# A two-layer attention and retention trunk on one core: gate chunk ahead of the attention, decay tiles two steps sooner, one up chunk in halves, and low weight parts from ScalarE and an accumulating DMA

## The chip, the core and the metric

The kernel runs on one core of a Trainium2 chip. The metric is the device time of the whole program in microseconds (us), as the median of several runs. Engines are named as in the profile: PE is TensorE (PEld is its weight load, which overlaps the matmuls), DVE is VectorE, ACT is ScalarE, POOL is GpSimd, and SP is SyncE, which here only issues DMAs.

## What is computed

Two layers work on a residual stream `h` of 512 tokens by 1024 features, all in float32. Cut to what matters, with the parts that the change touches in full width:

```python
u = rms_norm(h, norm_mix_pre[i])
qa, ka, va, qr, kr, vr, gr, gate_a, gate_b = split(u @ w_in[i])
att = dilated_attention_mixer(qa, ka, va)          # 8 heads of 64, softmax over banded keys
ret = retention_mixer(qr, kr, vr, gr, decay[i])    # 8 heads, decay matrix, group norm, silu(gr) gate
merged = sigmoid(gate_a) * (att @ w_att_out[i]) + sigmoid(gate_b) * (ret @ w_ret_out[i])
h = h + rms_norm(merged @ w_out[i], norm_mix_post[i])
u = rms_norm(h, norm_mlp_pre[i])
h = h + rms_norm(square(relu(u @ w_mlp_up[i])) @ w_mlp_down[i], norm_mlp_post[i])
gate = sigmoid(rms_norm(h) @ w_ple_gate[i])
h = h + gate * rms_norm(p[i] @ w_ple_proj[i], norm_ple[i])
```

## The kernel before

**Products in three terms.** Every float32 operand of a large product is split into a high part (a cast to the matmul's 32-bit format) and a low part (the operand minus its high part), and each product is the sum of high by high, high by low and low by high (`HL`, L292). Weights come as chunks of 128 by 1024 elements (512 KB) in the order of `PLAN_LAYER` (L69). `prefetch` (L268) loads a chunk into a `raw` tile over SP, casts the high part on ACT (L275), and takes the low part as a subtraction on DVE, or on POOL for two of three chunks of the kinds in `POOL_LOW` (the attention's and retention's q and k, retention's v, the gates `g` and `ga`, and the attention's output weights `ao`), as two instructions of 512 columns (L278). By the program there are 59 such chunks. `chunk` (L286) asks for the item three places ahead, and there are five `wt` buffers, so a tile's split can begin when PE starts the job four places ahead of its own.

**PE's order is written by hand.** PE executes in the order of the code; on DVE, ACT and POOL a scheduler sets the order by its own estimates and the priorities in `soon` (L372), and each engine then works strictly in that order. In the first half of a layer the main stream is a list of jobs, most of them 24 matmuls of 512 columns (`t_job`, L304): `rope_group` for q and k, `g_job` for the retention's gate, `vr_job`, `a_job` (gate of the attention and its output product), `b_gate`. The attention's and the retention's heads are a generator (`sides`, L728) that is advanced by `tick` (L469) at a rate of 0.94 for each 6 matmuls of the main stream; each `yield` is thus about one gap of 6 foreign matmuls. A head of the attention is four score steps (L543 to L550: PE, DVE, ACT's exponential, DVE's scaling of `z`), then the product of the head before (`pv`), then four steps of transposes of `z` (L562). A head of the retention is four score steps (L608 to L614), `finish` of the head before, the next head's decay tile `T` (`decay`, L581: POOL, then DVE, then ACT's exponential at L586), the product L630, its copy `yt` by ACT (L633), the transposes of `yt` on PE (L638) and the group norm on DVE and POOL.

**Norms.** `pre_norm` (L390) squares a token block of 128 (t0 to t3) on ACT (L348), takes the root on POOL (L356, L358), scales it on DVE (L404 or L407), and queues its transposes for PE: `step` (L322) emits them when the entry is `age` steps of 6 matmuls old, or `settle` does so when a product needs that block. ACT then casts the transposed block into `uT` (L415) and DVE makes the low part (L416). `AGE_DN` is the age in the down product. `EARLY` (L51) is how many chunks of the up product run as two halves of 256 token columns (L888), so that blocks t0 and t1 can start before t2 and t3 are normed.

The lines that the change touches most:

```python
AGE_DN = 6
EARLY = 3
            for sl in HALVES if pool else (slice(0, D),):
                low(nc.gpsimd if pool else nc.vector, t[:, 1, sl], r[:, sl], t[:, 0, sl])
```

## Time and profile before

| | before |
|---|---|
| median of 3 runs | 1790.33 us (1790.21 to 1791.44) |
| the profiled execution, whole | 1789.19 us |
| its span, first to last instruction | 1787.3 us |
| PE busy | 1771.2 us (99%) |
| DVE, ACT, POOL busy | 1138.5, 810.8, 374.9 us |
| granted TensorE clock | 1.000 |

PE is busy in nearly the whole span, so the time can only fall by PE's gaps or by matmuls that PE need not do. "Busy" counts from the start of a matmul to its modelled end, and neighbours overlap: 12 matmuls of 512 columns start 0.227 us apart, although one lasts 0.389 us. A wait shows its full length only between starts.

### The profile page before, as it was taken

What the parts mean: (1) busy time and instruction counts of PE and PEld (TensorE: products, weight loads), DVE (VectorE), ACT (ScalarE), POOL (GpSimd) and SP (SyncE); (2) the same over time, 40 slices, a digit from 0 to 9 for tenths busy, and PEclk for the clock granted to TensorE, in tenths of its full rate; (3) what the DMA queues carried; (4) which work ended last, traced back from release to release, by engine and by line L of the source; (5) the groups of instructions that cost most, each with busy time, mean ns of one, the idle gap of its engine ahead of it and who ended that gap; (6) DMA issues with size and microseconds to landing.
All of it is one profiled execution on the core that took longest, in us unless ns stands there. A gap on an engine that the chain in (4) does not pass through costs nothing.

```text
span 1787.3 us, 22085 instructions
## 1 busy us (share of the span) xinstructions
PE 1771.2 (99%) x8209; PEld 1465.5 (82%) x8209; DVE 1138.5 (64%) x1760; ACT 810.8 (45%) x1280; POOL 374.9 (21%) x346
## 2 busy tenths in 40 slices
PE   9999999999999999999999999999999999999998
PEld 7878888888898888888887888888888888888887
DVE  6677768743565677674656766677444657667754
ACT  5355554422466454433443555444234664444342
POOL 3321244311141001002123212443011410000030
PEclk9999999999999999999999999999999999999999
DMA  6554564552347566551346456556332566664411
GB/s 249 182 163 157 176 206 150 164 169 95 107 142 200 153 165 162 160 184 60 129 143 216 133 164 192 181 165 191 123 106 95 165 173 156 171 173 130 165 62 69
DMA packets 87951, 274.58 MB, mean 154 GB/s; under 512 B 11937, under 2 KB 20513, under 8 KB 87842
## 3 DMA queue, kind: packets, MB, share of 16 engines
q1 hardware_dynamic: 80930, 247.99, 41.4%
q0 software_dynamic: 6912, 25.17, 8.3%
q8 instruction: 65, 1.06, 0.2%
q14 instruction: 44, 0.36, 0.1%
HBM read 239.55 MB, written 33.55 MB: 153 GB/s over the span
## 4 chain that ended last, share of the span: by engine, by line
PE 91%; DVE 3%; POOL 2%; ACT 2%; DMA 1%; issue 1%; SPq 0%; POOLq 0%; ACTq 0%
PE acc L309 29%; PE acc L319 19%; PE s L309 18%; PE acc L866 9%; PE tp L866 4%; PE tp L630 2%; PE tp L525 2%; PE tp L562 2%; PE acc L888 1%; PE tp L412 1%; PE s L543 1%; PE s L608 1%; PE s L544 1%; PE s L609 1%; PE s L888 1%
## 5 line engine op out<-in xcount | busy, mean ns | idle before, releaser
L309 PE MATMUL acc<-uT,wt 128*128 128x512 f32 x1920 | 473.5, 393 | 0.0
L309 PEld LDWEIGHTS acc<-uT,wt 128*128 128x128 f32 x1920 | 355.8, 188 | 71.4
L298 DVE TENSOR_TENSOR wt<-raw,wt 128x1024 fp32r<-128x1024 f32 (+1 forms) x222 | 285.7, 1292 | 187.3 <-ACT wt L275 186.5
L275 ACT ACTIVATE wt<-raw 128x1024 fp32r<-128x1024 f32 x279 | 293.0, 1055 | 214.3 <-PE acc L309 109.1
L309 PE MATMUL s<-uT,wt 128*128 128x512 f32 x1392 | 323.7, 389 | 0.0
L319 PE MATMUL acc<-wt,uT 128*128 128x512 f32 x1320 | 319.0, 394 | 1.3 <-DVE wt L298 0.9
L309 PEld LDWEIGHTS s<-uT,wt 128*128 128x128 f32 x1392 | 261.1, 188 | 54.1
L319 PEld LDWEIGHTS acc<-wt,uT 128*128 128x128 f32 x1320 | 245.1, 188 | 52.6 <-DVE wt L298 2.3
L298 POOL TENSOR_TENSOR wt<-raw,wt 128x512 fp32r<-128x512 f32 x118 | 160.7, 1383 | 366.3 <-ACT wt L275 316.4
L866 PE MATMUL acc<-wt,op 128*128 128x512 f32 x672 | 159.5, 389 | 0.0
L866 PEld LDWEIGHTS acc<-wt,op 128*128 128x128 f32 x672 | 126.1, 188 | 26.2
L265 POOL DMA_DIRECT2D wsum<-in_w_dram x48 | 42.5, 891 | 418.9 <-DVE wt L298 140.2
L909 ACT ACTIVATE relu<-s 128x512 f32<-128x512 f32 x60 | 35.7, 594 | 182.9 <-PE s L309 173.6
L877 DVE TENSOR_TENSOR sumP<-acc,sumP 128x512 f32<-128x512 f32 x92 | 61.7, 686 | 56.8 <-PE acc L866 56.5
L309 PE MATMUL acc<-retT,wt 128*128 128x512 f32 x384 | 89.3, 389 | 0.0
L319 PE MATMUL acc<-wt,ff 128*128 128x512 f32 x384 | 88.5, 390 | 0.0
L298 DVE TENSOR_TENSOR wt<-wsum,wt 128x1024 fp32r<-128x1024 f32 x48 | 60.5, 1261 | 40.6 <-ACT wt L275 40.6
L309 PEld LDWEIGHTS acc<-retT,wt 128*128 128x128 f32 x384 | 72.1, 188 | 15.0
L319 PEld LDWEIGHTS acc<-wt,ff 128*128 128x128 f32 x384 | 71.8, 188 | 14.8
L301 ACT ACTIVATE rt<-rz 128x512 fp32r<-128x512 f32 x64 | 40.3, 631 | 91.2 <-DVE rz L612 91.0
L866 PE MATMUL tp<-wt,op 128*128 128x512 f32 x336 | 80.7, 389 | 0.0
L866 PEld LDWEIGHTS tp<-wt,op 128*128 128x128 f32 x336 | 63.1, 188 | 13.1
(164 smaller groups left out, 2149.2 us busy)
## 6 DMA issues: line engine op xcount, KB each, us to landing
raw<-in_w_dram SPq DMA_DIRECT2D x279, 512.0 KB, 3.7
wsum<-in_w_dram POOLq DMA_DIRECT2D x48, 512.0 KB, 5.5
kk<-stk SPq DMA_DIRECT2D x128, 128.0 KB, 4.5
wsum<-in_w_dram SPq DMA_DIRECT2D x24, 512.0 KB, 3.5
stq<-rr SPq DMA_DIRECT2D x16, 512.0 KB, 4.1
qs<-stq SPq DMA_DIRECT2D x128, 64.0 KB, 2.7
stk<-rr SPq DMA_DIRECT2D x16, 512.0 KB, 3.4
stv<-vr SPq DMA_DIRECT2D x16, 512.0 KB, 3.6
```

Source lines behind the costliest of these rows:

```text
L265: nc.gpsimd.dma_start(r, rows(src[1]), accum_op=ALU.add)
L275: nc.scalar.activation(t[:, 0, :], r, AF.Copy)
L298: eng.tensor_tensor(dst, src, hi.bitcast(F32), op=ALU.subtract)
L301: nc.scalar.activation(dst[:, 0], src, AF.Copy, scale=scale)
L309: nc.tensor.matmul(ps, lhsT=t[:, a, (off + k) * P:(off + k + 1) * P], rhs=r, start=k == 0 and n == 0, stop=k == kts - 1 and n == 2)
L319: nc.tensor.matmul(ps, lhsT=lhs(a, k, t), rhs=ch[:, b, j * S:(j + 1) * S], start=first and n == 0, stop=last and n == 2)
L525: nc.tensor.matmul(o, lhsT=v, rhs=pt[k][:, hl, :], start=k == 0 and hl == 0, stop=k == 3 and hl == 1)
L562: nc.tensor.transpose(ps[:, t * P:(t + 1) * P], zs[t][:, k * P:(k + 1) * P], ident)
L630: nc.tensor.matmul(o, lhsT=v[:, k, a * P:(a + 1) * P], rhs=rt[k][:, b, :], start=n == 0, stop=n == 11)
L866: nc.tensor.matmul(ps, lhsT=op[:, a, k, j * P:(j + 1) * P], rhs=t[:, b, k * S:(k + 1) * S], start=k == 0 and n == 0, stop=k == 1 and n == 2)
L877: nc.vector.tensor_tensor(a, ps, a, op=ALU.add)
L888: nc.tensor.matmul(early[c][:, 256 * j:256 * j + 256], lhsT=t[:, a, k * P:(k + 1) * P], rhs=uT[:, b, k, 256 * j:256 * j + 256], start=k == ...
```

## The change

Six edits:

- The low part of the 59 POOL chunks: ACT writes the negated cast of the weights into the low half of the tile, and a DMA issued by POOL adds the weights from HBM onto it. POOL's subtractions go, the chunks of DVE keep theirs.
- `g_job(0)` is called ahead of the start of the attention's generator, so 24 matmuls stand between the last rope product and the first score.
- Where an attention head has no earlier head to finish (head 0), one more `yield` is made.
- In the retention, `decay(h + 1)` is called at the second score step (k = 1) and no longer behind `finish`.
- `EARLY` goes from 3 to 1: the second and third up chunk run whole.
- `AGE_DN` goes from 6 to 7.

```diff
-AGE_DN = 6
+AGE_DN = 7
...
-EARLY = 3
+EARLY = 1
...
-            for sl in HALVES if pool else (slice(0, D),):
-                low(nc.gpsimd if pool else nc.vector, t[:, 1, sl], r[:, sl], t[:, 0, sl])
+            if pool:
+                nc.scalar.activation(t[:, 1, :], r, AF.Copy, scale=-1.0)
+                nc.gpsimd.dma_start(t[:, 1, :], rows(n).bitcast(F32R), accum_op=ALU.add)
+            else:
+                low(nc.vector, t[:, 1, :], r, t[:, 0, :])
...
             if late:
                 pv(*late)
+            else:
+                yield 1
...
                     qk, vh = load_qk(i, 1, h + 1), load_v(i, h + 1)
+                if k == 1 and h < 7:
+                    Tn = decay(h + 1)
                 yield 1
             if late:
                 finish(*late)
             yield 1
-            if h < 7:
-                Tn = decay(h + 1)
...
         rope_group(i, 0, 1, ca, "k")
+        g_job(0)
         side["gen"], side["rate"], side["owed"] = sides(), RATE, 0.0
...
         cr = cs_tile(1)
-        g_job(0)
         g_job(1)
```

Lines of the changed kernel stand 3 to 5 further down: L309 becomes L312, L348 L351, L404 L407, L415 L418, L416 L419, L543 L546, L562 L567, L586 L591, L633 L638; the negated cast is its L279 and the accumulating DMA its L280.

PE at head 0 of the attention in the first layer, from the last two score steps (L543, L544) to the first transposes (L562), before:

```order
L543 MATMUL s_81<-kk,qs 128x512
L544 MATMUL s_81<-kk,qs 128x512
L309 MATMUL acc_80<-uT,wt 128x512 x6
L543 MATMUL s_82<-kk,qs 128x512
L544 MATMUL s_82<-kk,qs 128x512
L309 MATMUL acc_80<-uT,wt 128x512 x12
L562 MATMUL tp_83<-ident,z 128x128 x4
```

And the same place in the changed kernel:

```order
L546 MATMUL s_81<-kk,qs 128x512
L547 MATMUL s_81<-kk,qs 128x512
L312 MATMUL acc_77<-uT,wt 128x512 x6
L546 MATMUL s_82<-kk,qs 128x512
L547 MATMUL s_82<-kk,qs 128x512
L312 MATMUL acc_77<-uT,wt 128x512 x18
L567 MATMUL tp_83<-ident,z 128x128 x4
```

Between the last score and the first transposes stand 18 foreign matmuls in place of 12.

ACT in the retention, from the third score's cast of a head (`rt`) to the copy `yt` that PE's transposes read, second head of the first layer, before:

```order
L301 ACTIVATE rt_2390<-rz_2388 128x512
L301 ACTIVATE rt_2404<-rz_2402 128x512
L301 ACTIVATE retT_2419<-yz_2417 128x512
L586 ACTIVATE T_2435<-T_2435 128x896
L633 ACTIVATE yt_2453<-tp1_84 128x512
```

And in the changed kernel, with the two casts of a chunk (L275, L279) ahead:

```order
L275 ACTIVATE wt_2551<-raw_2378 128x1024
L279 ACTIVATE wt_2551<-raw_2378 128x1024
L591 ACTIVATE T_2418<-T_2418 128x896
L304 ACTIVATE rt_2446<-rz_2444 128x512
L717 ACTIVATE tha_2449<-acc2_79 128x512
L304 ACTIVATE retT_2468<-yz_2466 128x512
L638 ACTIVATE yt_2490<-tp1_84 128x512
```

The decay tile's exponential no longer stands right ahead of `yt`; it is four places earlier, and a second cast has come in.

ACT in the down product of the first layer, second half: `un_6829` is the norm of block t1, `un_6885` that of t2, `junk` the square sum of t2, L275 casts of weights for the next product, and the casts into `uT` are first those of t0, then those of t1. Before:

```order
L415 ACTIVATE uT_88<-tp0_83 128x4x128
L415 ACTIVATE uT_88<-tp1_84 128x4x128
L348 ACTIVATE un_6829,ss_6831<-hr_6591 128x512
L348 ACTIVATE un_6829,ss_6834<-hr_6591 128x512
L348 ACTIVATE junk_6878,ss_6879<-sumP5_4440 128x512
L275 ACTIVATE wt_6755<-raw_6736 128x1024
L415 ACTIVATE uT_88<-tp0_83 128x4x128
L415 ACTIVATE uT_88<-tp1_84 128x4x128
L348 ACTIVATE un_6885,ss_6887<-hr_6593 128x512
L348 ACTIVATE un_6885,ss_6890<-hr_6593 128x512
```

And in the changed kernel, where `un_6781` is t1 and `un_6837` is t2:

```order
L351 ACTIVATE un_6781,ss_6783<-hr_6543 128x512
L418 ACTIVATE uT_88<-tp0_83 128x4x128
L351 ACTIVATE un_6781,ss_6786<-hr_6543 128x512
L418 ACTIVATE uT_88<-tp1_84 128x4x128
L351 ACTIVATE junk_6830,ss_6831<-sumP5_4440 128x512
L275 ACTIVATE wt_6707<-raw_6688 128x1024
L275 ACTIVATE wt_6718<-raw_6699 128x1024
L351 ACTIVATE un_6837,ss_6839<-hr_6545 128x512
L351 ACTIVATE un_6837,ss_6842<-hr_6545 128x512
L418 ACTIVATE uT_88<-tp0_83 128x4x128
L418 ACTIVATE uT_88<-tp1_84 128x4x128
```

The casts of t0 have moved between the halves of t1's norm, and those of t1 behind a second weight cast and the whole norm of t2.

DVE follows suit: at the same place the scaling of t1 (`un_6829`), then the square sum's operand of t2 (L950), the update of `h` for t2 (L943) and the low parts of t1's `uT`, before:

```order
L416 TENSOR_TENSOR uT_88<-tp1_84,uT_88 128x4x128
L404 TENSOR_SCALAR un_6829<-hr_6591,rstd_6836 128x512 x2
L950 TENSOR_TENSOR sumP5_4440<-acc0_77,sumP5_4440 128x512
L952 TENSOR_TENSOR sumP5_4440<-sumP5_4440,gain_4433 128x512
L943 SCALAR_TENSOR_TENSOR hr_6593<-sumP4_4444,rstd_6882,hr_6593 128x512
L943 SCALAR_TENSOR_TENSOR hr_6593<-sumP5_4440,rstd_6882,hr_6593 128x512
L416 TENSOR_TENSOR uT_88<-tp0_83,uT_88 128x4x128
L416 TENSOR_TENSOR uT_88<-tp1_84,uT_88 128x4x128
```

And in the changed kernel:

```order
L407 TENSOR_SCALAR un_6781<-hr_6543,rstd_6788 128x512 x2
L419 TENSOR_TENSOR uT_88<-tp1_84,uT_88 128x4x128
L955 TENSOR_TENSOR sumP5_4440<-acc2_79,sumP5_4440 128x512
L957 TENSOR_TENSOR sumP5_4440<-sumP5_4440,gain_4433 128x512
L948 SCALAR_TENSOR_TENSOR hr_6545<-sumP4_4444,rstd_6834,hr_6545 128x512
L948 SCALAR_TENSOR_TENSOR hr_6545<-sumP5_4440,rstd_6834,hr_6545 128x512
L301 TENSOR_TENSOR wt_6707<-raw_6688,wt_6707 128x1024
L301 TENSOR_TENSOR wt_6718<-raw_6699,wt_6718 128x1024
L407 TENSOR_SCALAR un_6837<-hr_6545,rstd_6844 128x512 x2
L419 TENSOR_TENSOR uT_88<-tp0_83,uT_88 128x4x128
L419 TENSOR_TENSOR uT_88<-tp1_84,uT_88 128x4x128
```

The low parts of t1's `uT` now stand behind two low parts of weights and the scaling of t2. The second layer has the same rows in the same order.

## Rows read from the trace of the kernel before

**Rows 1.** Page, part 1: busy us (share of the span), x instructions.
```profile
PE 1771.2 (99%) x8209; PEld 1465.5 (82%) x8209; DVE 1138.5 (64%) x1760; ACT 810.8 (45%) x1280; POOL 374.9 (21%) x346
```

**Rows 2.** Waits of PE, whole span: total us, times, longest.
```profile
PE tp L562 <- DVE z L550: 3.2, 4, 0.9
PE tp L638 <- ACT yt L633: 2.0, 5, 0.6
PE tp L412 <- DVE uT L416: 1.7, 2, 0.9
PE tp L412 <- DVE un L404: 1.6, 4, 0.6
...
PE s L543 <- DVE nm L547: 0.9, 2, 0.5
```

**Rows 3.** Timeline of PE, head 0, first layer: start, us, what, [idle before].
```profile
91.87 0.38 PE L562 MATMUL tp<-ident,z 128*128 128x128 f32 x2
...
94.42 1.64 PE L309 MATMUL acc<-uT,wt 128*128 128x512 f32 x6
95.89 0.60 PE L562 MATMUL tp<-ident,z 128*128 128x128 f32 x4
96.24 1.63 PE L309 MATMUL acc<-uT,wt 128*128 128x512 f32 x6
```

**Rows 4.** Timelines of DVE, then of POOL, there, and of DVE near 160.
```profile
89.93 0.48 DVE L550 TENSOR_SCALAR z<-z,rd 128x512 f32<-128x512 f32 x1
...
91.58 1.51 DVE L550 TENSOR_SCALAR z<-z,rd 128x512 f32<-128x512 f32 x1
...
90.19 2.61 POOL L298 TENSOR_TENSOR wt<-raw,wt 128x512 fp32r<-128x512 f32 x2 [4.74 <-ACT wt L275]
...
160.50 1.03 DVE L550 TENSOR_SCALAR z<-z,rd 128x512 f32<-128x512 f32 x1
```

**Rows 5.** Timelines of POOL and of ACT, second retention head.
```profile
259.00 3.00 POOL L298 TENSOR_TENSOR wt<-raw,wt 128x512 fp32r<-128x512 f32 x2 [1.27 <-ACT wt L275]
...
264.65 0.96 ACT L586 ACTIVATE T<-T 128x896 f32<-128x896 f32 x1 [0.83 <-DVE T L585]
```

**Rows 6.** Chain of waits, then timelines of PE and DVE: the up product.
```profile
526.02 5.76 PE acc L888 x48
...
548.12 5.44 PE s L309 x24
...
514.34 3.04 PE L888 MATMUL s<-uT,wt 128*128 128x256 f32 x24
...
515.61 1.29 DVE L416 TENSOR_TENSOR uT<-tp,uT 128x512 fp32r<-128x512 f32 x2 [0.82 <-ACT uT L415]
```

**Rows 7.** Timelines of PE, ACT and DVE: down product into gate product, first layer.
```profile
850.22 4.25 PE L319 MATMUL acc<-wt,uT 128*128 128x512 f32 x18
...
842.10 0.63 ACT L348 ACTIVATE un<-hr 128x512 f32<-128x512 f32 x1 [1.38 <-DVE hr L943]
...
848.05 1.06 ACT L415 ACTIVATE uT<-tp 128x512 fp32r<-128x512 f32 x2
...
844.62 0.88 DVE L404 TENSOR_SCALAR un<-hr,rstd 128x512 f32<-128x512 f32 x2 [0.69 <-POOL rstd L358]
845.41 0.69 DVE L950 TENSOR_TENSOR sumP<-acc,sumP 128x512 f32<-128x512 f32 x1
...
850.10 1.28 DVE L416 TENSOR_TENSOR uT<-tp,uT 128x512 fp32r<-128x512 f32 x2
```

**Rows 8.** Page, part 5, then parts 3 and 6 (DMA).
```profile
L275 ACT ACTIVATE wt<-raw 128x1024 fp32r<-128x1024 f32 x279 | 293.0, 1055 | 214.3 <-PE acc L309 109.1
...
q0 software_dynamic: 6912, 25.17, 8.3%
...
wsum<-in_w_dram POOLq DMA_DIRECT2D x48, 512.0 KB, 5.5
```

**Rows 9.** Windows: stretch, busy PE, PEld, DVE, ACT, POOL, clock, DMA share, GB/s.
```profile
100.00:370.00 270.00, 268.66 (x1266) 220.76 (x1265) 198.04 (x403) 130.81 (x216) 86.56 (x66) 1.00 0.56 174
```

## The prediction

> **What bounds the kernel now.** I read part 1 of the page first: PE is busy in 1771.2 of 1787.3 us [rows 1], so 16.1 us of the span are not PE's, and part of these is the start, ahead of the first matmul. DVE at 64%, ACT at 45% and POOL at 21% set no pace of their own; they matter only where PE waits for one of their results. So I read the waits of PE next [rows 2]: five kinds, 9.4 us as idle time. Then the timelines around each kind, start to start, because a wait shows shortened in the idle column: a matmul lasts longer in the record than the pitch to the next. Everything below is either a wait of that list, a matmul that PE need not do, or a new wait.
>
> **Head 0 of the attention (g_job ahead, one more yield).** Four transposes and the step to the next matmul take 96.24 - 95.89 = 0.35 us when nothing is missing; at head 0 they take 94.42 - 91.87 = 2.55 us [rows 3]. That is 2.2 us lost to `z` of the third and fourth score step. The wait for L550 comes four times, two in each layer, 3.2 us as idle time [rows 2]; the first layer's 2.2 us against its share of that (about 1.75) gives 4.0 us for both layers. In the changed order 18 foreign matmuls stand ahead of the transposes in place of 12, so 6 x 0.227 = 1.36 us more cover; and 24 matmuls (5.44 us) now lie between the last rope product and the first score, so DVE has its rope work behind it. Of the 2.2 us, 1.03 us is one scaling that took 1.51 us and not 0.48 while POOL's subtraction ran (90.19 to 92.80) [rows 4]; that subtraction is gone. 1.36 + 1.03 = 2.39 is over 2.2, without counting the rope work. So the wait goes: **-4.0 us**, bounds -4.1 and -2.0 (half of it stays).
>
> By the Trainium skill, page "SBUF — State Buffer", section "SBUF: two separate sides", VectorE in a two-port mode and GpSimd exclude each other for a whole instruction. The stretched scaling agrees (1.51 against 0.48 us). By that rule the 1.03 us goes for certain, and only the rest of this term hangs on the order.
>
> The moved jobs cost nothing by themselves: the same matmuls in another place, no DMA among them. The generator starts 4 ticks nearer the end of the job list and has one yield more, 5 ticks in all. By the code it needs 134 advances and gets 148 x 0.94 = 139, so it still ends within the list, and the products that read its results start 5 ticks (some 7 us) later.
>
> **Decay tile two steps sooner.** PE waits five times for `yt`, 2.0 us idle [rows 2]. In the one shown, ACT runs the exponential of the next decay tile at 264.65, after 0.83 us of waiting for DVE; `yt` comes right behind it in ACT's order, and the tile was late because POOL came to it only after a subtraction of 3.00 us [rows 5]. In the order of before the exponential stands right ahead of `yt`; in the changed one it is four places earlier. Four of the five waits have that exponential as ACT's last step before `yt`. Start to start the five are about 1.4 times their idle time, 2.8 us; four fifths give **-2.2 us**. Bounds: -2.8 and 0, because a cast or a `retT` now stands ahead of `yt` and can be late as the exponential was.
>
> **POOL's subtractions gone.** Besides head 0, PE waits twice for L547, 0.9 us idle [rows 2], 1.2 us start to start by the same factor; in the first layer another scaling there took 1.03 us and not 0.48 [rows 4]. I take **-0.8 us**, bounds -1.2 and 0.
>
> **What the negated cast and the DMA cost.** 59 casts of 1.055 us [rows 8] are 62 us more for ACT, all in the two first halves of layers, where ACT is busy in 130.8 of 270 us [rows 9]. The DMAs run beside them. For the tile itself there is room: 1.06 + 1.06 + 5.5 us to landing [rows 8] is 7.6 us, and a split begins four jobs ahead, 4 x 5.44 = 21.8 us. The issue on POOL waits for the second cast as the subtraction waited for the first; queued behind it on POOL are the low part of `rt`, the decay tile and the root of the group norm, and POOL's own work for a chunk falls. SP's `raw` buffer comes free after the second cast, earlier than after two subtractions. What costs is ACT's queue: work that PE waits for may stand behind a cast. Nearest row: before, 279 casts of the same length run there [rows 8], and the only wait of PE on ACT in the list is `yt`, 2.0 us. That gives less than 0.01 us for a cast; all 59 exposed would give 62 us. ACT gets denser, so I take near the low end, but well above it, **+1.0 us**, bounds 0 and +8.
>
> **One up chunk in halves.** A chunk in 48 halves takes 5.76 us, a whole one in 24 takes 5.44 [rows 6]. Two chunks in each of two layers become whole: 4 x 0.32 = **-1.3 us**. What hid the late blocks was 3 x 2.88 = 8.64 us of first halves; now it is 2.88. The halves start at 514.34, so blocks t2 and t3 are read from 517.22. Their last low parts are done at 515.61 + 1.29 = 516.90 [rows 6]. The cover is still there, with 0.3 us left; if they come 1 us later, 0.7 us of this goes back in each layer (bounds -1.3 and +0.5).
>
> **AGE_DN 7.** This looks like the smallest edit and is the largest unknown. The waits for L404 and L416 are 3.3 us [rows 2], about 4.4 us start to start in two layers. The transposes of t0 and t1 come one step (1.36 us) later in the down product. I walk the new orders of ACT and DVE with the times of before, first layer.
> The norm of t1 starts at 842.10 as before [rows 7], but ACT casts t0 between its two halves, which ends them 0.65 us later; the scaling (L404) goes from 844.62 to 845.3. PE wants t1 at 845.5 and waits 0.3 us, and 0.55 us more for its second bank, which DVE frees after that scaling at 846.7. So t1 waits about as before; t0's wait is gone.
> Behind it L950 of t2 moves from 845.41 to 846.7, and t2's square sum on ACT ends at 848.2. Then ACT has two weight casts (to 850.2), the norm of t2 (to 852.1), and only then the casts of t1, at 852.1 and not 848.05 [rows 7]. DVE has the update of `h` (to 851.1), two low parts of weights (to 853.4), the scaling of t2 (to 854.2), and only then the low parts of t1: first half done at 854.9, where before both were done by 851.4.
> PE starts the gate product at about 849.95 (850.22 before) and needs t1 at 851.3 + 0.45. It waits 3.1 us. In return the wait for t3 (0.9 us idle, 1.1 start to start) has nothing left to wait for, since t3's chain moves only 2 us. Against before: +3.1, -1.1, t0 -0.35, t1 +0.1; with the shift of the start that is 1.55 us for a layer, **+3.1 us** for two. Bounds: -4.4 (all these waits vanish) and +6.2 (3.1 us in each layer, nothing given back).
>
> **Sum.** -4.0 - 2.2 - 0.8 + 1.0 - 1.3 + 3.1 = -4.2 us, on the profiled execution 1787.3 to 1783.1 of span. The median of the runs stands 3.0 us above that span (1790.33), so **1786.1 us**. A measurement of this kernel can tell about 0.2%, 3.6 us, from no change; the forecast lies just beyond it.
>
> **The rivals.**
> *The gate product doesn't wait.* If t1 arrives in time (the weight casts find their buffers late and are passed over in time, or DVE is faster), the +3.1 falls to 0 or below: -7.3 to -8.5, about **1782.4 us**. For it: only about 0.8 us of earlier arrival for each place in the queue is needed. Against it: the order is strict, and three rows of it follow one another.
> *The head's wait only moves.* The change does not do what it says: the first head's transposes are fed, and PE waits the same time at the next head or at the end of the list. Then -0.2 us, **1790.1 us**. For it: DVE is at 198 of 270 us there [rows 9]. Against: later heads have a product of 8 matmuls and two gaps more as cover, and show no such wait [rows 2].
> *The accumulating DMAs crowd the queues*, and the kernel is slower. 48 of them took 8.3% of 16 engines' time [rows 8], 3.1 us each; 59 are 182 us, in about 680 us of first halves, so the DMA share there goes from 0.56 [rows 9] to 0.83. A chunk's load then lands later; ACT waits for it in its strict order, and the exponentials, `pt` and `yt` stand behind. It decides from the point where a load lands later than one job of the main stream with its side work (about 8 us; 3.7 before, q0's 5.5) after its issue. If one in six of the 59 added chunks then holds ACT for 1.4 us on PE's path, that is +14 us: **1800 us**. Against: loads have two chunks of lead, and no wait of PE for a DMA stands in the list [rows 2].
>
> **How the numbers follow.** Forecast 0.50, no wait in the gate product 0.25, wait only moved 0.10, crowded queues 0.15. The forecast's own spread is about 2 us on either side, so 0.29 of its 0.50 is faster by over 0.2% and 0.21 within. Of the second rival 0.24 is faster; of the third all but 0.01 within; of the fourth 0.11 slower, 0.04 within. Together: faster 0.53, within 0.2% 0.35, slower 0.12. The range from 1781.5 to 1791.0 holds the forecast, most of the second rival and the third, and leaves out the worst of the fourth and the lower end of the second.
>
> **What would show it.** Right: no wait of PE for L550's line at head 0; at most one or two for `yt`; 24 whole matmuls of up chunks 1 and 2 with no wait ahead of t2's half; in the gate product one wait of some 3 us for L416's line in each layer, and none for t3. Wrong: PE waiting for `wt` or a DMA in the first halves, ACT idle on `raw` loads, a DMA share far over 0.8 with late `kk`; or the gate product starting without a wait, which would make the time lower than forecast.

## The result and the profile after

The changed kernel takes 1802.41 us (median of 4 runs, 1797.88 to 1805.4) against 1790.27 us for the kernel before in the same comparison: a ratio of 1.0065, with a 95% interval from 1.0042 to 1.0089. It is 12 us slower, where 4 us faster was forecast. The profiled execution is the fastest of the four, 1797.88 us with a span of 1796.1 us, so 4.5 us of the median are not in this trace.

Page of the changed kernel, part 1, which answers to [rows 1]; then its DMA queue of POOL and two kinds of transfer (parts 3 and 6: packets, MB, share of 16 engines; KB each, us to landing):

```profile
PE 1775.3 (99%) x8113; PEld 1463.9 (82%) x8113; DVE 1109.1 (62%) x1760; ACT 864.8 (48%) x1339; POOL 269.0 (15%) x287
...
q0 software_dynamic: 15408, 56.11, 17.8%
...
wt<-in_w_dram POOLq DMA_DIRECT2D x59, 512.0 KB, 8.3
...
kk<-stk SPq DMA_DIRECT2D x128, 128.0 KB, 5.7
```

The edits did what they say: POOL has lost 106 us, ACT has gained 54, and PE has 96 matmuls fewer (48 halves for 24 whole ones, four times). PE is busy for 4 us longer nevertheless.

Waits of PE in the changed kernel, whole span (total us, times, longest), which answer to [rows 2]:

```profile
PE acc L322 <- DVE uT L419: 5.3, 3, 2.5
PE s L613 <- DMA kk<-stk: 2.8, 2, 1.5
PE acc L322 <- ACT uT L418: 1.9, 2, 0.9
PE tp L567 <- DVE z L553: 1.4, 2, 0.7
...
PE tp L599 <- DVE y L653: 1.2, 2, 0.6
```

The waits that the change aimed at are gone or small: `z` at head 0 (what is left of L567 lies at the third head), L543, and `yt`, which has one wait of 0.2 us. In their place stand three others: the gate product for `uT` (L322), the retention's first score for `kk` (L613), and the last head's transposes for `y` (L599).

The gate product of the first layer in the changed kernel, timelines of PE, ACT and DVE (start, us, what, [idle before]), which answer to [rows 7]:

```profile
849.41 1.52 PE L322 MATMUL acc<-wt,uT 128*128 128x512 f32 x6
851.86 0.73 PE L322 MATMUL acc<-wt,uT 128*128 128x512 f32 x2 [0.93 <-ACT uT L418]
855.08 3.59 PE L322 MATMUL acc<-wt,uT 128*128 128x512 f32 x10 [2.48 <-DVE uT L419]
...
847.43 1.99 ACT L275 ACTIVATE wt<-raw 128x1024 fp32r<-128x1024 f32 x2
...
851.23 1.07 ACT L418 ACTIVATE uT<-tp 128x512 fp32r<-128x512 f32 x2
...
850.43 2.35 DVE L301 TENSOR_TENSOR wt<-raw,wt 128x1024 fp32r<-128x1024 f32 x2
...
854.34 1.28 DVE L419 TENSOR_TENSOR uT<-tp,uT 128x512 fp32r<-128x512 f32 x2
```

This is the walk of the prediction, line by line: two weight casts and the norm of t2 ahead of t1's casts on ACT, two low parts of weights and the scaling of t2 ahead of t1's low parts on DVE. PE starts at 849.41 (849.95 by the walk) and goes on at 855.08 (854.9), when the first of t1's two low parts is done. The six first matmuls and two more take 8 x 0.227 = 1.8 us of these 5.67, so the wait is 3.9 us against the 3.1 of the walk.

What the walk had not asked is what TensorE does afterwards. Windows of the changed kernel around the gate product of each layer (busy us of PE, PEld, DVE, ACT, POOL; then the granted clock, DMA share, GB/s):

```profile
850.00:856.00 6.00, 2.59 (x11) 1.50 (x10) 5.23 (x8) 4.19 (x8) 2.00 (x2) 1.00 0.47 154
856.00:860.00 4.00, 4.00 (x17) 3.32 (x16) 3.23 (x5) 1.22 (x3) 1.47 (x2) 0.57 0.45 154
1739.00:1744.00 5.00, 2.29 (x9) 1.24 (x8) 4.24 (x7) 4.38 (x9) 2.00 (x2) 0.99 0.32 106
1744.00:1751.00 7.00, 6.27 (x19) 5.22 (x20) 6.23 (x10) 2.19 (x6) 1.47 (x2) 0.52 0.46 149
```

Behind each wait the granted clock is at its lower level, 1.2 and not 2.4 GHz, for most of 4 us in the first layer and of 7 us in the second, although PE is busy there. At that level PE loses 4 x 0.43 = 1.7 us of its busy time in the first layer and 6.27 x 0.48 = 3.0 us in the second, where 0.7 of the 7 us are the end of the wait itself: 4.7 us for both layers. The Trainium skill, page "TensorE: Matmul & The Clock Gate", section "What's actually happening", has the same two levels, set by how busy PE has been lately; the rows agree, and no row of the kernel before could show it, since the longest of its waits in [rows 2] is 0.9 us as idle time.

### The profile page after: what moved, and what is told of

Read it like the earlier page. It is cut to its first block, busy times and chain, and to the rows that moved or that the text cites. A ratio compares the mean times of both kernels' runs of the same rounds, so it can differ in the third digit from the quotient of the medians.

```text
span 1796.1 us, 21951 instructions
## 1 busy us (share of the span) xinstructions
PE 1775.3 (99%) x8113; PEld 1463.9 (82%) x8113; DVE 1109.1 (62%) x1760; ACT 864.8 (48%) x1339; POOL 269.0 (15%) x287
## 3 DMA queue, kind: packets, MB, share of 16 engines
q0 software_dynamic: 15408, 56.11, 17.8%
## 4 chain that ended last, share of the span: by engine, by line
PE 90%; DVE 3%; ACT 2%; DMA 2%; issue 1%; POOL 1%; SPq 1%; ACTq 0%; POOLq 0%; DVEq 0%
PE acc L312 28%; PE acc L322 20%; PE s L312 19%; PE acc L871 8%; PE tp L871 4%; PE tp L635 2%; PE tp L567 1%; PE tp L528 1%; PE tp L415 1%; DMA kk<-stk 1%; PE s L546 1%; PE s L547 1%; PE s L613 1%; PE s L614 1%; PE s L893 1%
## 5 line engine op out<-in xcount | busy, mean ns | idle before, releaser
L312 PE MATMUL acc<-uT,wt 128*128 128x512 f32 x1920 | 473.2, 393 | 0.0
L312 PEld LDWEIGHTS acc<-uT,wt 128*128 128x128 f32 x1920 | 355.8, 188 | 71.5
L275 ACT ACTIVATE wt<-raw 128x1024 fp32r<-128x1024 f32 x279 | 293.2, 1056 | 217.8 <-PE acc L312 93.7
L312 PE MATMUL s<-uT,wt 128*128 128x512 f32 x1488 | 345.5, 389 | 0.0
L322 PE MATMUL acc<-wt,uT 128*128 128x512 f32 x1320 | 323.0, 397 | 8.4 <-DVE uT L419 5.3
L312 PEld LDWEIGHTS s<-uT,wt 128*128 128x128 f32 x1488 | 279.2, 188 | 57.9
L322 PEld LDWEIGHTS acc<-wt,uT 128*128 128x128 f32 x1320 | 246.3, 190 | 61.6 <-DVE uT L419 6.8
L280 POOL DMA_DIRECT2D wt<-in_w_dram x59 | 52.5, 890 | 450.9 <-ACT wt L279 376.4
L312 PE MATMUL acc<-retT,wt 128*128 128x512 f32 x384 | 89.3, 389 | 0.0
L322 PE MATMUL acc<-wt,ff 128*128 128x512 f32 x384 | 88.4, 390 | 0.0
L312 PEld LDWEIGHTS acc<-retT,wt 128*128 128x128 f32 x384 | 72.1, 188 | 15.0
L322 PEld LDWEIGHTS acc<-wt,ff 128*128 128x128 f32 x384 | 71.8, 188 | 14.7
```

The costliest lines, as they stand in the source:

```text
L275: nc.scalar.activation(t[:, 0, :], r, AF.Copy)
L280: nc.gpsimd.dma_start(t[:, 1, :], rows(n).bitcast(F32R), accum_op=ALU.add)
L312: nc.tensor.matmul(ps, lhsT=t[:, a, (off + k) * P:(off + k + 1) * P], rhs=r, start=k == 0 and n == 0, stop=k == kts - 1 and n == 2)
L322: nc.tensor.matmul(ps, lhsT=lhs(a, k, t), rhs=ch[:, b, j * S:(j + 1) * S], start=first and n == 0, stop=last and n == 2)
```

## Experiments

All ratios are to the kernel before, measured beside each, whose median was 1789.8 to 1790.6 us in these comparisons. Theory A at first: the late block t1, with the clock behind it, is the loss. Theory B, the fourth rival of the prediction: the accumulating DMAs are.

**One edit undone.** In `e1_age6`:

```diff
-AGE_DN = 7
+AGE_DN = 6
```

> The changed kernel with AGE_DN back at 6. Theory A (the late block t1 and the clock behind it): with 7, PE waits 3.7 us for t1 in the gate product of each layer, and the granted clock is at 0.5 for some 3.3 us behind it in the first layer and 6.7 us in the second. With 6 both go: the waits fall by about 2 x 2.4 us, the clock gives back about 4.6 us, so 1802.4 becomes 1793, and 1789 if the spread of the runs above the profiled one was clock loss as well. Theory B (the accumulating DMAs crowd the queues of the two first halves and cost most of it): the waits there are not touched, so the time stays at 1797 or above.

In `e2_poolsub`:

```diff
-            if pool:
-                nc.scalar.activation(t[:, 1, :], r, AF.Copy, scale=-1.0)
-                nc.gpsimd.dma_start(t[:, 1, :], rows(n).bitcast(F32R), accum_op=ALU.add)
-            else:
-                low(nc.vector, t[:, 1, :], r, t[:, 0, :])
+            for sl in HALVES if pool else (slice(0, D),):
+                low(nc.gpsimd if pool else nc.vector, t[:, 1, sl], r[:, sl], t[:, 0, sl])
```

> The changed kernel with POOL's subtractions in place of the negated cast and the accumulating DMA; AGE_DN stays 7. Theory A: only the new waits of the first halves can go, 5.6 us in sum, so 1797 us, and the clock still falls behind the gate product. Theory B: most of the 12 us goes, 1792 us or below.

`e3_age6_poolsub` has both diffs.

> Both undone: what is left is the gate chunk ahead, the yield of head 0, the early decay tile and one up chunk in halves. By the terms that I gave these three (-4.0, -2.2, -1.3) 1783 us. Theory A and B agree on about 1784 to 1787; if it is 1790 or more, the waits that the first halves gained come from the moved jobs themselves and not from the DMAs.

Measured: 1794.13 us with AGE_DN 6 (ratio 1.0022, 1.0012 to 1.0031), 1799.42 us with POOL's subtractions (1.0050, 1.0036 to 1.0063), 1791.61 us with both (1.0009, 1.0000 to 1.0018). AGE_DN 7 thus costs 8.3 us with the DMAs and 7.8 us without them. By the medians the DMAs cost 3.0 and 2.5 us; the intervals overlap in both pairs, so these two figures are weak, and only their agreement speaks for them. Theory A is right for the largest part, theory B at most for a small one. And the three edits that are left, to which the prediction gave -7.5 us, come out at +1.8 us.

**The edit by itself.** `e12_age7` is the kernel before with AGE_DN 7.

> The kernel before with AGE_DN 7 and nothing else. The pair with POOL's subtractions gave 7.8 us for it, so 1797.9, with 3.7 us of waits for t1 in the gate product of each layer and a granted clock of 0.5 behind each of them. If the wait needs the other edits (one up chunk in halves, another order of the weight chunks), 1790 to 1792.

Measured: 1800.27 us (1.0049, 1.0036 to 1.0061), so 9.7 us for the one number. The wait needs none of the other edits.

**Is it the standstill that brings the clock down?** `e4_filled` is the changed kernel with 18 matmuls (`row_mm` makes three each time) into a spare bank behind the first six of the gate product:

```diff
+                    if keys[0][1:] == ("pg", 0) and c == 0 and t == 0:
+                        spare = bank("s")
+                        for m in range(6):
+                            row_mm(spare, chs[0], 0, lhs, 0, t, m == 0, m == 6 - 1)
```

> The changed kernel, with 18 more matmuls of 512 columns (4.1 us) into a spare bank behind the first six of the gate product in each layer, so that PE works through the 3.7 us in which it waited for t1. They compute nothing that is used. If the clock falls because PE stands still there, the granted clock stays at 1.00 and the time falls by 3 to 8 us although the work has grown by 8.2 us: 1795 to 1799. If the fall has another reason, the clock falls as before, and the time is 1802 to 1804.

Measured: 1797.47 us (1.0040, 1.0028 to 1.0053), 4.9 us less than the changed kernel by the medians, with 8.2 us more of matmuls. The time alone is weak evidence: the two intervals overlap, four of the five runs lie below all runs of the changed kernel, and the two traces are 1.6 us apart. The clock is read from the trace. Timeline of PE in this kernel, then windows, at the same places:

```profile
852.28 1.52 PE L322 MATMUL acc<-wt,uT 128*128 128x512 f32 x6
853.64 4.24 PE L322 MATMUL s<-wt,uT 128*128 128x512 f32 x18
```

```profile
856.00:862.00 6.00, 6.00 (x32) 5.06 (x31) 4.83 (x8) 1.78 (x4) 1.83 (x3) 1.00 0.58 187
1738.00:1746.00 8.00, 8.00 (x37) 6.62 (x36) 6.08 (x9) 6.49 (x12) 3.35 (x4) 1.00 0.26 86
```

The block t1 is as late as before, PE works through the wait, and the clock stays at 1.00. So the fall comes from the standstill. The fill itself gains nothing, as it is longer (8.2 us) than PE had waited there (2 x 3.9); what can be won by it is the clock's part, 4.7 us.

**The other edits one by one, on the kernel before.** `e5_head0` has the gate chunk ahead and the yield; `e6_yield` the yield alone; `e7_decay` the early decay tile; `e8_neg` the negated cast with the DMA. Their diffs are those parts of the change.

> The kernel before with the gate chunk ahead of the attention and the yield of head 0, and nothing else changed. Theory A2 (the moved job shifts the heads against the rope products, so that head 0's wait goes, 4.2 us, and head 1 meets the rope work of the retention's q on DVE, with 2 x 1.9 us at its last transposes and up to 1.8 us at scores): 1789 to 1791, no gain. Rival (the new waits at head 1 come from the other edits): 1786, the -4.0 of my sum.

> The kernel before with the one yield of head 0 alone; the gate chunk stays where it was. It gives the transposes 6 matmuls, 1.36 us, more cover, of the 2.1 and 1.9 us that they waited, and shifts the later heads by one gap and not by five. If the cover counts: -2.5 us, 1787.3. If one gap of shift already moves heads into rope work: 1789 or above.

> The kernel before with the decay tile at the second score step, and nothing else. By my term the five waits for yt (2.8 us) fall by 2.2 us: 1787.6. Rival (the tile's work on POOL and DVE now stands ahead of the low parts of rt, and the product L630 waits for these): 1789 to 1790, with waits for rt in place of yt.

> The kernel before with the negated cast and the accumulating DMA in place of POOL's subtractions, and nothing else. The difference of the changed kernel with and without them was +2.5 to +3.0 us, so 1792.5, with waits for kk whose transfer from DRAM lands late. Rival (these waits come from the shifted order; by itself the DMA takes the stretched scalings and the L547 waits away): 1789, or below.

| | us | ratio, interval | prediction's term |
|---|---|---|---|
| `e5_head0` | 1793.67 | 1.0020, 1.0011 to 1.0029 | -4.0 |
| `e6_yield` | 1793.00 | 1.0014, 1.0005 to 1.0022 | part of it |
| `e7_decay` | 1796.99 | 1.0034, 1.0021 to 1.0046 | -2.2 |
| `e8_neg` | 1784.94 | 0.9972, 0.9961 to 0.9982 | -0.8 + 1.0 |

`e5_head0` and `e7_decay` lie above both answers of their expectations, `e6_yield` and `e8_neg` agree with the second one. The cast with the DMA is the only one of them that wins, and the two edits that were to bring the most lose by themselves. With the yield alone (`e6_yield`) the waits for `z` fall from 3.2 to 1.0 us, but those for `yt` grow from 2.0 to 3.8 and one of 2.4 us for `y` in two comes up; behind the first layer's `y` the clock is 0.59 from 369 to 373 us.

Waits of PE with head 0's edits alone (`e5_head0`), first against [rows 2]:

```profile
PE tp L564 <- DVE z L550: 3.8, 3, 1.7
PE tp L640 <- ACT yt L635: 2.0, 3, 1.1
PE s L543 <- DVE nm L547: 1.9, 4, 0.5
...
PE tp L596 <- DVE y L650: 1.2, 2, 0.6
```

Not one of the three waits for `z` is at head 0. Timeline of PE and DVE of the same kernel at the third head of the attention, where two of them lie, one in each layer (by a miscount the expectations call it head 1; counted from 0 it is head 2). L494 to L497 are rope work of a product of the retention:

```profile
136.29 0.49 PE L564 MATMUL tp<-ident,z 128*128 128x128 f32 x3
138.49 0.33 PE L564 MATMUL tp<-ident,z 128*128 128x128 f32 x1 [1.71 <-DVE z L550]
...
131.46 0.69 DVE L494 TENSOR_TENSOR ra<-acc,cst 128x512 f32<-128x512 f32 x1
...
132.76 1.47 DVE L550 TENSOR_SCALAR z<-z,rd 128x512 f32<-128x512 f32 x1
...
135.95 0.67 DVE L547 CUSTOM_DVE_ANT_0 z<-s,lct 128x512 f32<-128x512 f32 x1
```

Before, this head's last score left PE at 126.0 and the first of these rope steps came at 129.52, behind the last scaling. Now the last score comes at 131.3, its L547 stands behind five rope steps (131.46 to 136), and one scaling is stretched from 0.48 to 1.47 us by a subtraction of POOL (131.38, 2.57 us).

For the decay tile by itself (`e7_decay`), timelines of POOL, DVE and PE at one of the new waits, then a window behind it (columns as above):

```profile
352.28 1.06 POOL L265 DMA_DIRECT2D wsum<-in_w_dram  x1 [12.38 <-DMA wsum<-in_w_dram]
353.09 1.32 POOL L646 TENSOR_TENSOR rs<-ve,neghalf 128x4 f32<-128x4 f32 x1
354.45 0.41 DVE L648 TENSOR_SCALAR y<-tp,mv,rs 128x128 f32<-128x128 f32 x1 [5.77 <-POOL rs L646]
354.77 0.68 DVE L612 TENSOR_TENSOR rz<-s,T 128x512 f32<-128x512 f32 x1
355.51 0.52 PE L608 MATMUL s<-qs,kk 128*128 128x512 f32 x1 [1.94 <-DVE rz L612]
...
356.00:358.00 2.00, 2.00 (x7) 1.52 (x6) 2.00 (x5) 0.75 (x2) 1.30 (x1) 0.50 0.59 115
```

POOL stands for 12.4 us ahead of the issue of an accumulating DMA whose tile hasn't landed; the group norm's root waits behind it, DVE behind that, and PE behind DVE. Behind PE's wait the clock is at 0.50 from 356 to 358 us and at 0.68 on average from 358 to 360, so 1.6 us more are lost. The kernel before has the same issue with the root behind it, after 8.4 us (346.91 and 347.73), and no wait of PE there; why the early decay tile makes that load later isn't shown. Besides, five waits for low parts of `rt` on DVE (2.0 us) and two for its casts on ACT (1.1 us) have come; that the tile's 1.14 us on DVE, which now stand among them, make them is not tested. The waits for `yt` fell from five to one.

In `e8_neg` the waits for L550's line fell from four, 3.2 us, to one of 0.8 us, and those for L547 are gone. Timeline of DVE and PE of this kernel at head 0, against [rows 4]:

```profile
91.52 0.48 DVE L553 TENSOR_SCALAR z<-z,rd 128x512 f32<-128x512 f32 x1
...
93.43 0.60 PE L565 MATMUL tp<-ident,z 128*128 128x128 f32 x4
```

The scaling that took 1.51 us beside POOL's subtraction takes 0.48 us without it, and the four transposes run in one piece. This is what the rule in the Trainium skill's "SBUF — State Buffer" (section "SBUF: two separate sides") leads one to expect. The waits for `z` and L547 are 3.3 us shorter as idle time, the other waits of the list 0.9 us longer (among them a new one for `kk`, 0.6 us). The trace is of one of the slower runs, 2.6 us of span ahead of the kernel before; the median's gain of 5.1 us, which the prediction had put at next to nothing, is only in part in it.

**Edits together.** `e9_neg_early1` is `e8_neg` with `EARLY = 1`; `e10_neg_early1_decay` has the early decay tile as well; `e11_neg_early1_head0` is `e9_neg_early1` with head 0's edits.

> The kernel before with the negated cast and accumulating DMA, and with one up chunk in halves: the two edits whose terms the runs so far bear out. 1784.9 less the 1.3 us of the two whole chunks in each layer: 1783.6. If the cover of the halves is too short, a wait ahead of the second half gives it back: 1785.

> The same two edits and the decay tile at the second score step. By itself that step cost 6.9 us. Theory P (it cost that because POOL's subtractions stand between the tile and the work behind it): with POOL free of them 1783 to 1785. Theory V (VectorE's 1.14 us for the tile stands ahead of the low parts that the product waits for, whatever POOL does): 1787 to 1790, with waits for rt.

> The same two edits, with the gate chunk ahead and the yield of head 0. By itself that step cost 3.6 us with POOL's subtractions. If the cost is head 1 meeting the rope work, it is less without the stretched scalings (0.9 in place of 1.9 us in each layer), 1785; if the shift also brings loads of kk behind accumulating DMAs, 1788 to 1791 with runs several us apart, as in the changed kernel. Together with the decay tile this is the changed kernel at AGE_DN 6, 1794.1.

Measured: 1783.77 us (0.9961, 0.9949 to 0.9974), **1781.45 us (0.9950, 0.9936 to 0.9964)**, and 1791.60 us (1.0003, 0.9994 to 1.0012). The halves bring 1.2 us. The decay tile, which cost 6.9 us beside POOL's subtractions, brings 2.3 us without them, as theory P of its expectation had it, and more than it gave. The waits for `rt` and the score's bank that the tile brought by itself are not in this trace. Waits of PE in `e10_neg_early1_decay`, the fastest kernel, down to 0.8 us:

```profile
PE tp L415 <- DVE uT L419: 1.6, 2, 0.8
PE tp L415 <- DVE un L407: 1.6, 4, 0.6
PE acc L322 <- DVE wt L301: 1.3, 2, 0.8
PE s L237 <- DVE warm L233: 1.0, 1, 1.0
PE tp L565 <- DVE z L553: 0.8, 1, 0.8
```

It has three of the six edits, and is 9 us faster than the kernel before and 21 us faster than the changed one. Of the waits that the change aimed at, one of 0.8 us is left in this list; the others are those of the down product, which AGE_DN 6 keeps, and the start. Head 0's edits cost 7.8 us on `e9_neg_early1` and, from 1781.45 to the 1794.13 of `e1_age6`, 12.7 us on the fastest one. The trace of `e1_age6` is of its fastest run (1790.41 us). It is 9.2 us longer than the fastest kernel's, with PE's waits 5.2 us longer as idle time, some 7 us start to start by the prediction's factor of 1.4: for `rt` 2.0 us, for `kk` 1.9, for `y` at the end of the list 1.2 and for `z` 0.6 us more, and 0.5 us less elsewhere.

**Which part of head 0's edits costs?** On the fastest kernel, the yield alone (`e13_best_yield`), the gate chunk alone (`e14_best_gate`), and both with the third gate chunk put ahead of the rope product of q, in the order of the weight chunks (`PLAN_LAYER`) too (`e15_best_reordered`):

```diff
...
+        g_job(2)
         rope_group(i, 1, 0, cr, "q")
-        g_job(2)
```

> The fastest kernel so far (negated cast and DMA, one up chunk in halves, early decay tile: 1781.45) with the yield of head 0 added. One gap of shift. If any shift of the heads against the main list costs, 1783 to 1786, with waits at other heads; if only the moved gate chunk costs, 1781 (0.9 us of head 0's wait in the second layer is all that can still be won).

> The fastest kernel so far with the gate chunk ahead of the attention and no yield: four gaps of shift. The two edits together cost 12.7 us on top of it (the changed kernel at AGE_DN 6, 1794.1). If the cost is the phase of the heads against rope work and against the loads of kk, 1788 to 1793, with waits for z at head 1 and for kk at the first retention head. If the yield is the larger part, 1783 to 1786.

> The fastest kernel so far with both edits of head 0, and with the third gate chunk ahead of the rope product of the retention's q in place of behind it, so that this rope work meets the heads where it did before (one gap apart). Theory (rope work on DVE in the middle of head 1's scores makes the waits at 100 to 250 us and 1000 to 1130 us, some 3.5 us in each layer): these waits fall by half or more, and the time goes from 1794 to 1787 to 1790. Rival (the heads only are late at the end of the list, and wait for kk): they stay, 1792 to 1796.

Measured: 1786.87 us (0.9981, 0.9972 to 0.9990), 1798.43 us (1.0045, 1.0033 to 1.0058), 1793.63 us (1.0015, 1.0004 to 1.0025). One gap of shift costs 5.4 us, four gaps 17.0, five 12.7: the cost does not grow with the shift. The first two are above every range of their expectations; the third is in that of the rival. With the yield alone, the largest wait is for `y` at the end of the list (2.4 us in two). With the gate chunk alone it is for `z` and `y`, with 4.1 us more for `pt` and `part`; waits of PE in `e14_best_gate`:

```profile
PE tp L565 <- DVE z L553: 5.5, 4, 1.7
PE tp L597 <- DVE y L651: 3.7, 2, 1.9
```

In the reordered kernel the wait for `z` at the third head stayed, 0.6 us as idle time in each layer, which spoke against the rope work as its cause. But by counting the jobs of the list up to 131 us, the rope work that this head meets is that of k, not of q: the experiment had moved the wrong one.

**The right rope product, and `kk`.** On `e1_age6`: the fourth gate chunk ahead of the rope product of k, and in the order of the weight chunks too (`e16_k_later`), and the load of the retention's first q and k asked for in the last head of the attention (`e17_kk_early`):

```diff
...
+        g_job(3)
         rope_group(i, 1, 0, cr, "k")
-        g_job(3)
```

```diff
-                if t == 0 and h < 7:
-                    qk = load_qk(i, 0, h + 1)
+                if t == 0:
+                    qk = load_qk(i, 0, h + 1) if h < 7 else load_qk(i, 1, 0)
...
```

> The changed kernel at AGE_DN 6 (1794.1), with the fourth gate chunk ahead of the rope product of the retention's k in place of behind it. Counting jobs of the main list, the rope work that meets head 1 at 131 us is that of k, not of q; with one job more ahead of it, it lies at 139 us, as before the change. If it makes the wait for z at head 1 (0.9 us in each layer), that goes, and 1790 to 1793 stays for the waits for kk, rt and y. If the wait stays, rope work isn't its cause, and the time is 1794.

> The changed kernel at AGE_DN 6, with the load of the first retention head's q and k asked for one head earlier, in the last head of the attention, in place of at the retention's start. If the wait for kk (1.1 to 1.6 us in the profiled runs, and the most of the 8 us by which the runs differ) comes from its place behind other transfers on SP's queue, it goes: 1789 to 1791, runs within 3 us. If the loads are late because the queues are full, whatever their place: 1793 or more with the same spread.

Measured: 1794.38 us (1.0020, 1.0011 to 1.0029) and 1793.43 us (1.0018, 1.0009 to 1.0027). In `e16_k_later` the waits for `z` at the third head are gone in both layers: k's rope work is the cause of those. The time has not moved. Its trace, of a run at the median, has as PE's largest wait:

```profile
PE s L613 <- DMA kk<-stk: 4.5, 2, 3.1
```

Behind the wait of 3.1 us the clock is 0.50 from 1130 to 1134 us. The trace of `e1_age6` has 1.9 us for `kk`, but it is of its fastest run, 3.7 us below the median; whether the edit made these waits longer or they differ from run to run isn't shown. Where they come from is seen on SP. Timelines of SP, first in `e9_neg_early1`, without the shift, then in the changed kernel:

```profile
218.92 1.76 SPq L696 DMA_DIRECT2D stv<-vr  x2
...
225.37 4.11 SPq L516 DMA_DIRECT2D kk<-stk  x6
```

```profile
231.34 1.95 SPq L698 DMA_DIRECT2D stv<-vr  x2
...
233.34 3.00 SPq L516 DMA_DIRECT2D kk<-stk  x4
```

With the shift, the loads of `kk` stand behind stores of `vr`, whose product isn't there before 231. They start 8 us later, while PE wants the tile 6.7 us later (at 241.4, not 234.7), and they land more slowly: in the stretch from 200 to 245 us the median of the `kk` loads is 7.7 us in the changed kernel and 2.9 us in the fastest one. The last part lands at 243 (chain of waits of the changed kernel, start, us, what):

```profile
235.61 7.40 DMA kk<-stk
```

Asked for earlier (`e17_kk_early`), no wait for `kk` is left in the trace, which is again that of the fastest run (1789.89 us). Waits for `rt` (2.4 us in all, 2.0 in `e1_age6`) and for a score's bank (0.6 us) are there, and the 0.7 us by which the median fell are within the spread. Neither edit alone makes the shift worth its price; the two together were not run.

Where PE stands for 2 to 3 us, the clock is at stake again. Windows of `e14_best_gate` behind its two waits for `y`, second layer and first, 3.7 us together, the longer one 1.9 us as idle time:

```profile
1262.00:1266.00 4.00, 2.14 (x10) 1.10 (x8) 2.61 (x7) 0.00 (x0) 1.04 (x1) 1.00 1.06 275
1266.00:1270.00 4.00, 4.00 (x12) 3.16 (x12) 1.39 (x2) 0.63 (x1) 0.00 (x0) 0.58 0.33 130
...
372.00:376.00 4.00, 2.15 (x10) 1.32 (x8) 2.84 (x9) 0.22 (x1) 1.03 (x1) 1.00 1.04 320
376.00:380.00 4.00, 4.00 (x18) 3.07 (x18) 1.98 (x4) 0.84 (x2) 0.00 (x0) 1.00 0.74 225
```

The same wait was followed by a fall in one layer and not in the other. A fall follows waits of 1.9 us in `e7_decay`, 2.6 us in `e11_neg_early1_head0` (0.58 from 1130 to 1132 us) and 3.1 us in `e16_k_later`, all as idle time. It fits that runs of one kernel differ where it has such waits: `e1_age6` lies between 1790.4 us (granted clock 0.999 to 1.000) and 1798.4 us (0.998), the fastest kernel between 1781.3 and 1782.3 us, all at 1.000.

**One step more.** `e18_best_pg` is the fastest kernel with `"pg"` added to `POOL_LOW`:

> The fastest kernel so far (1781.45), with the negated cast and the accumulating DMA for two of three chunks of the last gate product too. It takes low parts of 1.2 us out of DVE's order where blocks t0 to t3 wait in the down and gate products (4.1 us in two layers). If a low part stands in the way of each: 1779 to 1780.5. If the casts on ACT or the DMA's landing take its place: 1781.5 or more.

Measured: 1800.97 us (1.0056, 1.0043 to 1.0070). PE waits for the tile itself, and again with the clock behind it (0.995 over the run):

```profile
PE acc L322 <- DMA wt<-in_w_dram: 15.4, 4, 7.7
```

In the first halves of the layers a tile's split has a lead of 21.8 us by the prediction; at the start of the gate product the tile's DMA was issued at 848.29 and took 8.9 us, while PE had started that product at 846.4.

## Why the prediction was wrong

Two terms of the sum failed in the changed kernel: AGE_DN 7 and, with the largest error, head 0.

- **AGE_DN 7.** The mechanism, its place and its order of events were right: the first half of t1's low parts ends at 855.0 (854.9 forecast), t3's wait is gone, t1's own transposes wait about as long as before. But the wait is 3.9 and not 3.1 us in each layer, and the step that failed outright is that a wait was priced as the time in which PE stands. Behind it TensorE runs at half its clock, another 4.7 us for both layers in the profiled execution. The two waits and the clock, less the walk's 2.9 us for t0 and t3, give 7.7 + 4.7 - 2.9 = 9.5 us. Measured: +8.3 us in the changed kernel, +9.7 alone; forecast +3.1, bound +6.2. (The walk's own items add up to 1.75 us for a layer, 3.5 for two: the 1.55 counts the earlier start, which t0 and t1 make, a second time in part.) The first rival (no wait in the gate product) has fallen.
- **Head 0.** Its own wait went as the step said: none is left there. The step that failed is the sentence that the moved jobs cost nothing by themselves. It looked at the jobs (the same matmuls, no DMA) and at the end of the generator, and not at what else the heads meet when they run five gaps later: k's rope work on DVE at the third head, the stores of `vr` on SP ahead of `kk`, the group norm at the end. That is the rival that the wait only moves, which had a chance of 0.10; it was too mild, since what it moved to cost more: -4.0 forecast, +3.6 us alone, +7.8 and +12.7 us on faster kernels. Which of the meetings costs how much is open: with the wait for `z` at the third head gone, or that for `kk`, the median moved by 0.7 us at most.
- **Decay tile.** `yt`'s waits went as forecast, and -2.3 us against -2.2 is right where POOL is free and the heads stay in place. Beside POOL's subtractions it costs 6.9 us, and with the shift of head 0 2.5 us by the medians (from `e11_neg_early1_head0` to `e1_age6`). The bound of 0 above was wrong: it let a cast be late ahead of `yt`, and forgot that the tile's own steps on POOL and DVE move ahead of `rt`.
- **POOL's subtractions and the negated cast.** Taken together (the stretched scaling of head 0 is in another term) these were too cautious: by themselves -5.1 us. The rival of crowded queues is there in the landings (`kk` 5.7 us against 4.5 before, DMAs of POOL 17.8% against 8.3% of 16 engines in [rows 8]); the DMA share from 100 to 370 us is 0.75, where it gave 0.83. But the fastest kernel has the same (`kk` 6.0 us, 18.2%) and no wait of PE for a DMA in its trace, so crowding by itself isn't the loss. The 2.5 to 3.0 us that the DMAs cost in the changed kernel fit the lead that the shift takes from the loads. That the time came out near that rival's 1800 us is luck, not its doing.
- **One up chunk in halves.** -1.2 us measured, -1.3 forecast, no wait ahead of the second half.
- **The range.** Its upper end, 1791.0, lies below what the upper bound of one term alone gives (the casts at +8: 1793.1 us), head 0's term had no bound above zero, and no term had one for what a long wait does to the clock.

From the kernel before, the edits add up in this order to the changed kernel: cast and DMA -5.1, halves -1.2, decay tile -2.3, head 0 +12.7, AGE_DN +8.3, together +12.4 us; +12.1 was measured. As each step starts where the one before ends, the sum has to come out; in another order the steps would have other sizes (head 0 alone: +3.6).

Still open: the trace of `e17_kk_early` has no wait for `kk`, and its runs are 6 us apart all the same (granted clock 0.998 to 1.000). The slower runs have a lower clock; which wait decides it from run to run is not shown, since only the fastest run has a trace.

## What to carry to other kernels

Price a new wait of TensorE by its length and by what the clock does behind it: waits of 3.9 us cost 1.7 and 3.0 us more, a wait of 2.0 us cost 1.7 us more in one layer and nothing in the other, and harmless matmuls in the place of the wait kept the clock up. Moving work of one stream against another is an edit of every meeting of the two, so list what lies on each queue (VectorE, POOL, SP) at the new offsets, for every later head and not only the first. Test edits alone and in pairs: here the early decay tile changed sign with the edit that freed POOL, and a bundle of six that lost 12 us held three that win 9 us.

## What the runs showed of the hardware

In the changed kernel an accumulating DMA of 512 KB from HBM onto a tile took 8.3 us (median) from its issue to landing, against 4.0 us for a plain load of the same size by SP. In `e14_best_gate` the granted clock fell behind a wait of 2.0 us between starts in one layer and not behind its twin in the other. A VectorE scaling of 0.48 us took 1.03 to 1.51 us beside a subtraction of POOL, and 0.48 us at head 0 where POOL only issued DMAs.
